# One of the experts' activation instructions moved from VectorE to ScalarE, and a slot's gate read as one sum

## The chip, the cores and the metric

The kernel runs on one core of a Trainium2 chip. Its time is the device time of that core, in microseconds (us). Three runs of the kernel before took 3082.26, 3086.06 and 3087.57 us; the median is 3086.06.

## The reference

Two transformer blocks over 512 tokens of width 1024, in float32. The first block mixes by attention and ends in a mixture of experts; the second block (two layers) mixes by three branches. The change lies in the experts of the first block. Each token is routed to 4 of 32 experts, and only the chosen ones count:

```python
def expert_block(args):
    xblk, e = args
    gu = xblk @ w_gate_up[e] + b_gate_up[e]
    gate = jnp.minimum(gu[:, :D_FF], SWIGLU_LIMIT)
    up = jnp.clip(gu[:, D_FF:], -SWIGLU_LIMIT, SWIGLU_LIMIT)
    act = (up + 1.0) * (gate * jax.nn.sigmoid(SWIGLU_ALPHA * gate))
    return act @ w_down[e] + b_down[e]
```

The limit is 7 and alpha 1.702. Each expert's result is scaled by the token's gate, a softmax over its four logits, and added to that token's row. The weights are 1024 x 2048 (gate and up) and 1024 x 1024 (down) per expert.

## The kernel before

**Products in split precision.** The matrix unit takes float32 rounded to a shorter mantissa. So every operand is split into a high part (a copy on ScalarE, line 49) and a low part (the rest, a subtraction on VectorE, line 50), and a product is three matmuls: high times low, low times high, high times high (lines 82 to 84). Each weight piece of 1 MB (`raw`, 128 x 2048) is loaded by a queue of SyncE, split into `whi` and `wlo`, and used by 12 matmuls of 512 columns. There are 8 buffers of `raw` and 4 each of `whi` and `wlo`, so `whi` of a piece can be made when the piece four places before has been used up.

**An expert.** Up to 96 token slots (NS) are served per expert. `place(e)` finds an expert's tokens: a one-hot matrix `poh` (line 765), four small matmuls and a sum give the row numbers `gi` (lines 777, 778), and four more matmuls with `VG`, which holds each gate as a high and a low part, give the two parts of every slot's gate in one PSUM tile `T` (line 782). Lines 784 and 785 bring the two parts to SBUF and add them into `gate`, which scales the expert's result much later (line 911). `gather` brings the tokens' rows, `prep` transposes and splits them. `gate_up(e, h, x)` computes one half of the hidden columns, 512 of them: `ps[0]` is the gate's product, `ps[1]` the up product, each of two weight pieces, each a PSUM bank `G` of its own begun by one bias matmul (line 849). Then comes the activation on 96 x 512 elements, and its result is transposed (line 892) and split for `down(e, h, ...)`, which multiplies it with two further weight pieces into two banks `Y`. An expert thus takes twelve pieces.

**The activation.** sigmoid is taken as half of 1 + tanh, and the half is put in at the split of the result. ScalarE computes relu(7 − gate) from `ps[0]` and from that the tanh; both take their constant from a column of a small tile `c7`. VectorE does four instructions: it bounds `up` (line 886), bounds the gate into a tile `gm` (line 887), computes (tanh + 1) times `gm` (line 888), and (up + 1) times that (line 889).

**Order.** The loop over experts writes `gate_up(e, 0)`, then `prep`, `gather` and `place` for later experts, then `down(e − 1, 1)`, `gate_up(e, 1)` and `down(e, 0)`. Each engine runs its instructions in a fixed order, but that order is not the written one: a planner goes through the program with its own account of time and gives an engine, whenever it comes free, the instruction that is ready and stands first in the program. The order of the whole program is planned anew whenever the program changes. The same function that reads the gates (`slots`) serves the overflow path, which runs only if an expert has more than 96 tokens.

Of the kernel before, what the change touches and what calls it, by code (L numbers as in the profile page):

```python
# [9 lines left out]
F32 = mybir.dt.float32  # L10
# [4 lines left out]
AF = mybir.ActivationFunctionType  # L15
ALU = mybir.AluOpType
AX = mybir.AxisListType
# [12 lines left out]
NS = 96  # L30
# [4 lines left out]
def f(t):  # L35
    return t.bitcast(F32)


class Kern:
# [729 lines left out]
    def slots(self, bank, oh, V, vg, gi, gate):  # L769

        nc = self.nc
        n = oh.shape[-1]
        p = bank[:n, :4]

        def find():
            for i in range(NT):
                nc.tensor.matmul(p[:, :2], lhsT=oh[:, i], rhs=V[:, i], start=i == 0, stop=i == NT - 1)
            return nc.vector.tensor_scalar(gi[:n], p[:, 0:1], BASE, self.spare[:n], op0=ALU.add, op1=ALU.min).ins

        def gates():  # L780
            for i in range(NT):
                nc.tensor.matmul(p[:, 2:], lhsT=oh[:, i], rhs=vg[:, i], start=i == 0, stop=i == NT - 1)
            g = self.small.tile([128, 2], F32, name="g2")
            nc.vector.tensor_copy(g[:n], p[:, 2:])
            nc.vector.tensor_add(gate[:n], g[:n, 0:1], g[:n, 1:2])
        return find, gates

    def gather(self, e):
# [4 lines left out]
    def moe_setup(self):  # L793

        nc, tc, a = self.nc, self.tc, self.a
        FF = 1024
        T = dict(reuse_waits="tile")
        self.ms = ExitStack()
        mc = self.mc = self.ms.enter_context(tc.tile_pool(name="mc", bufs=1, **T))
        xg = self.xg = [mc.tile([NS, D], F32, name=f"xg{n}") for n in range(2)]  # L800
        for t in xg:
            nc.gpsimd.memset(t, 0.0)
        self.mraw = self.ms.enter_context(tc.tile_pool(name="mraw", bufs=NE, **T))

        bias = self.bias = mc.tile([128, FF], F32R, name="bias")
        bt = self.mraw.tile([128, 2048], F32, name="bt", tag="raw")[:, :FF]
        for r in (0, 32):
            nc.sync.dma_start(bt[r:r + 32], a["b_gate_up"][:, :FF])  # L810
            nc.sync.dma_start(bt[64 + r:96 + r], a["b_gate_up"][:, FF:])
        nc.scalar.activation(bias, bt, AF.Copy)
        for r in (32, 96):
            nc.vector.tensor_sub(bias[r:r + 32], bt[r:r + 32], f(bias)[r:r + 32])

        esel = self.esel = mc.tile([128, 2, 32], F32R, name="esel")
        nc.gpsimd.memset(f(esel), 0.0)
        for r in range(0, 128, 32):
            nc.vector.tensor_copy(esel[r:r + 32, r // 64], self.ident[r:r + 32, r:r + 32])
        c7 = self.c7 = mc.tile([128, 2], F32, name="c7")  # L820
        nc.vector.memset(c7[:, 0:1], 7.0)
        nc.vector.memset(c7[:, 1:2], 0.851 * 7.0)
        self.gi = mc.tile([128, 32], I32, name="gi")
        self.gate = mc.tile([128, 32], F32, name="gate")

# [7 lines left out]
    def moe(self, ctx):  # L833


        nc, tc, a, mc = self.nc, self.tc, self.a, self.mc
        esel, bias, c7, xg = self.esel, self.bias, self.c7, self.xg
# [4 lines left out]
        mp = P("mp", 2, **T)  # L842
        self.wp, self.wk = (self.mraw, P("mhi", 4, **T), P("mlo", 4, **T)), 4
        psG, psY, psT = P("psG", 4, space=PSUM, **T), P("psY", 2, space=PSUM, **T), P("psTm", 2, space=PSUM, **T)
        gi, gate, gather = self.gi, self.gate, self.gather
        wgu, wdn = a["w_gate_up"], a["w_down"]

        def add_bias(ps, e, c):
            nc.tensor.matmul(ps, lhsT=esel[:, c // 2, e:e + 1].to_broadcast([128, NS]),
                             rhs=bias[:, c % 2 * 512:c % 2 * 512 + 512], start=True, stop=False)  # L850
# [20 lines left out]
        def gate_up(e, h, x):  # L871
            xh, xl = x
            ps = []
            for c in (h, 2 + h):
                W = self.weight(wgu[e, :, c * 512:c * 512 + 512], KT, 512)
                p = psG.tile([128, 512], F32, name="G")[:NS]
                add_bias(p, e, c)
                self.mm3(p, [((xh[:, k], xl[:, k]), W[k]) for k in range(KT)], start=False)
                ps.append(p)
            s = mp.tile([NS, 512], F32, name="sg", bufs=3)  # L880

            nc.scalar.activation(s, ps[0], AF.Relu, scale=-1.0, bias=c7[:NS, 0:1])
            nc.scalar.activation(s, s, AF.Tanh, scale=-0.851, bias=c7[:NS, 1:2])
            u = mp.tile([NS, 512], F32, name="up", bufs=3)
            g = mp.tile([NS, 512], F32, name="gm", bufs=2)
            nc.vector.tensor_scalar(u, ps[1], 7.0, -7.0, op0=ALU.min, op1=ALU.max)
            nc.vector.tensor_scalar(g, ps[0], 7.0, None, op0=ALU.min)
            nc.vector.scalar_tensor_tensor(s, s, 1.0, g, op0=ALU.add, op1=ALU.mult)
            self.act_dve = nc.vector.scalar_tensor_tensor(u, u, 1.0, s, op0=ALU.add, op1=ALU.mult).ins
            p = psT.tile([128, 512], F32, name="T", tag="T")[:, :4 * NS].rearrange("p (k s) -> p k s", k=4)  # L890
            for k in range(4):
                nc.tensor.transpose(p[:, k], u[:, k * 128:(k + 1) * 128], self.ident[:NS, :NS])
            th = mp.tile([128, 4, NS], F32R, name="ath", bufs=3)
            tl = mp.tile([128, 4, NS], F32R, name="atl", bufs=3)
            self.split(th, tl, p, 0.5)
            return th, tl
# [53 lines left out]
        for e in range(E):  # L950
            acts[e, 0] = gate_up(e, 0, x[e])
            if e + 1 < E:
                x[e + 1] = prep(e + 1)
                if e + 2 < E:
                    gather(e + 2)
                if e + 3 < E:
                    place(e + 3)
            if e == E - 4:
                gates_T()
            if e == E - 2:  # L960
                one_hot()
            if e:
                down(e - 1, 1, acts[e - 1, 1])
            acts[e, 1] = gate_up(e, 1, x[e])
            if e < E - 1:
                down(e, 0, acts[e, 0])
# [7 lines left out]
        g = gate[:NS, E - 1:E]  # L974
# [558 lines left out]
```

## Time and profile before

| | |
|---|---|
| median of three runs | 3086.06 us |
| the profiled execution | 3086.88 us |
| its span, first to last instruction | 3085.1 us |
| PE (TensorE's matmuls) busy | 2917.6 us, 95% |
| DVE (VectorE) busy | 2250.2 us, 73% |
| ACT (ScalarE) busy | 1737.4 us, 56% |
| mean granted clock of TensorE | 0.982 |

The experts' stage lies between about 700 and 1860 us of the span. In the rows, PE is the matmul engine and PEld its weight loads, and an instruction is written as what it writes, an arrow, and what it reads. L82 is line 82 of the kernel. A number in square brackets at the end of a timeline row is the idle time of the engine before it, with what ended the idle time. Times in a timeline row are the start and the duration in us. Consecutive instructions of one engine overlap a little, so the step from start to start is shorter than the duration.

### The profile page before, as it was taken

To read this page: it belongs to the slowest core of one execution; us is meant where nothing else is said; L and a number is where in the kernel's file an instruction comes from. 1 tells how busy PE (TensorE), PEld (TensorE's weight loads), DVE (VectorE), ACT (ScalarE), POOL (GpSimd) and SP (SyncE) were. 2 spreads that over 40 slices of the span, in tenths; PEclk is the share of its full clock that TensorE was granted. 3 is DMA by queue.
4 is the path that set the end of the run, shared out by engine and by line. 5 is a ranking of instruction groups with operands and counts; after the bars stand their busy time and mean duration, and the time that the engine had idled before them with its cause. 6 is when DMAs were issued, how large, how long until landed. Compare 5 with 4: busy or idle time off the path is not lost.

```text
span 3085.1 us, 39468 instructions
## 1 busy us (share of the span) xinstructions
PE 2917.6 (95%) x14226; PEld 2293.6 (74%) x14226; DVE 2250.2 (73%) x3789; ACT 1737.4 (56%) x2577; POOL 318.4 (10%) x316
## 2 busy tenths in 40 slices
PE   7999999979999999999999997999999979999998
PEld 6898878766777666666666665878887868888876
DVE  7765577668998999999999997554466585445664
ACT  5555545337777777777777774444454234444532
POOL 0000001001112111111111101011000020110000
PEclk9999999989999999999999999999999989999999
DMA  5122233469999999999999994433536433345262
GB/s 157 63 69 67 76 107 96 129 257 318 366 365 345 354 352 360 355 359 361 356 359 359 349 368 129 133 102 114 113 103 202 148 98 115 112 118 114 89 235 89
DMA packets 405833, 644.92 MB, mean 209 GB/s; under 512 B 23024, under 2 KB 150528, under 8 KB 405632
## 3 DMA queue, kind: packets, MB, share of 16 engines
q1 hardware_dynamic: 385808, 581.67, 56.6%
q0 software_dynamic: 19248, 58.58, 6.4%
q8 instruction: 114, 1.87, 0.3%
q10 hardware_dynamic: 576, 2.10, 0.2%
q14 instruction: 87, 0.71, 0.1%
HBM read 592.10 MB, written 54.36 MB: 210 GB/s over the span
## 4 chain that ended last, share of the span: by engine, by line
PE 74%; DVE 12%; issue 7%; ACT 3%; DMA 3%; SPq 0%; POOL 0%; POOLq 0%; ACTq 0%; DVEq 0%
PE M L82 6%; PE M L83 6%; PE G L82 6%; PE M L84 6%; PE G L84 6%; PE G L83 6%; PE F L82 5%; PE F L83 5%; PE F L84 5%; DVE wlo L50 5%; PE Y L82 4%; PE Y L83 3%; PE Y L84 3%; DMA raw<-in_w_in 1%; PE O L82 1%
## 5 line engine op out<-in xcount | busy, mean ns | idle before, releaser
L50 DVE TENSOR_TENSOR wlo<-raw,whi 128x2048 fp32r<-128x2048 f32 (+4 forms) x642 | 1161.9, 1821 | 274.0 <-ACT whi L49 269.8
L49 ACT ACTIVATE whi<-raw 128x2048 fp32r<-128x2048 f32 (+3 forms) x646 | 972.1, 1532 | 231.3 <-PE M L84 110.3
L82 PE MATMUL G<-wlo,exh 128*96 128x512 f32 x1024 | 410.0, 400 | 4.7 <-ACT exh L49 2.7
L83 PE MATMUL G<-whi,exl 128*96 128x512 f32 x1024 | 404.0, 395 | 1.9 <-DVE exl L50 1.9
L84 PE MATMUL G<-whi,exh 128*96 128x512 f32 x1024 | 403.8, 394 | 0.0
L82 PE MATMUL F<-xl,whi 128*128 128x512 f32 x768 | 311.3, 405 | 17.1 <-DVE fl L1228 10.0
L83 PE MATMUL F<-xh,wlo 128*128 128x512 f32 x768 | 305.3, 398 | 2.3 <-DVE wlo L50 2.3
L84 PE MATMUL F<-xh,whi 128*128 128x512 f32 x768 | 305.6, 398 | 0.0
L82 PE MATMUL M<-wlo,xh 128*128 128x512 f32 (+2 forms) x736 | 278.1, 380 | 12.4 <-POOL wlo L50 3.5
L83 PE MATMUL M<-whi,xl 128*128 128x512 f32 (+2 forms) x736 | 275.2, 374 | 0.0
L84 PE MATMUL M<-whi,xh 128*128 128x512 f32 (+2 forms) x736 | 274.0, 374 | 0.0
L84 PEld LDWEIGHTS G<-whi,exh 128*96 128x96 f32 x1024 | 165.7, 162 | 71.5
L82 PEld LDWEIGHTS G<-wlo,exh 128*96 128x96 f32 x1024 | 165.8, 162 | 70.6 <-ACT exh L49 3.0
L82 PE MATMUL Y<-wlo,ath 128*96 128x512 f32 x512 | 207.4, 405 | 10.6 <-DVE wlo L50 9.9
L83 PEld LDWEIGHTS G<-whi,exl 128*96 128x96 f32 x1024 | 165.7, 162 | 67.3 <-DVE exl L50 2.4
L83 PE MATMUL Y<-whi,atl 128*96 128x512 f32 x512 | 202.4, 395 | 0.1
L84 PE MATMUL Y<-whi,ath 128*96 128x512 f32 x512 | 201.8, 394 | 0.0
L82 PEld LDWEIGHTS M<-wlo,xh 128*128 128x128 f32 x736 | 164.4, 223 | 32.9 <-DVE wlo L50 4.9
L82 PEld LDWEIGHTS F<-xl,whi 128*128 128x128 f32 x768 | 146.0, 190 | 54.9 <-DVE fl L1228 13.5
L83 PEld LDWEIGHTS M<-whi,xl 128*128 128x128 f32 x736 | 165.0, 224 | 13.6
L84 PEld LDWEIGHTS M<-whi,xh 128*128 128x128 f32 x736 | 164.4, 223 | 14.1
L83 PEld LDWEIGHTS F<-xh,wlo 128*128 128x128 f32 x768 | 146.2, 190 | 32.0 <-DVE wlo L50 3.0
(479 smaller groups left out, 5095.3 us busy)
## 6 DMA issues: line engine op xcount, KB each, us to landing
raw<-in_w_gate_up SPq DMA_DIRECT2D x256, 1024.0 KB, 7.0
raw<-in_w_down SPq DMA_DIRECT2D x124, 1024.0 KB, 8.2
raw<-in_w_in SPq DMA_DIRECT2D x154, 512.0 KB, 4.0
GZ<-fl POOLq DMA_DIRECT2D x80, 256.0 KB, 2.4
raw<-in_w_out SPq DMA_DIRECT2D x24, 512.0 KB, 3.9
raw<-in_w_branch SPq DMA_DIRECT2D x24, 512.0 KB, 4.4
gt<-GZ SPq DMA_DIRECT2D x48, 256.0 KB, 3.1
raw<-in_w_in SPq DMA_DIRECT2D x32, 256.0 KB, 3.1
```

The lines of the kernel that those rows point to most:

```text
L49: self.last_act = nc.scalar.activation(hi, src, AF.Copy)
L50: self.last_dve = (eng or nc.vector).tensor_sub(lo, src, f(hi))
L82: nc.tensor.matmul(out, lhsT=ah, rhs=bl, start=start and i == 0, stop=False)
L83: nc.tensor.matmul(out, lhsT=al, rhs=bh, start=False, stop=False)
L84: self.last_mm = nc.tensor.matmul(out, lhsT=ah, rhs=bh, start=False, stop=stop and i == n - 1)
```

## The change

The 1 of 1 + tanh is added by a third instruction on ScalarE (an Identity with the constant 1 as its bias, a new column of `c7`). VectorE bounds the gate and multiplies it with 1 + tanh in one instruction, which reads `ps[0]` itself; the tile `gm` is gone. The activation has three instructions on ScalarE and three on VectorE, where it had two and four. In `slots` the two parts of a gate are summed in one instruction that reads PSUM, instead of a copy and an addition.

```diff
@@ -780,9 +780,7 @@
         def gates():
             for i in range(NT):
                 nc.tensor.matmul(p[:, 2:], lhsT=oh[:, i], rhs=vg[:, i], start=i == 0, stop=i == NT - 1)
-            g = self.small.tile([128, 2], F32, name="g2")
-            nc.vector.tensor_copy(g[:n], p[:, 2:])
-            nc.vector.tensor_add(gate[:n], g[:n, 0:1], g[:n, 1:2])
+            nc.vector.reduce_sum(gate[:n], p[:, 2:], axis=AX.X)
         return find, gates
@@ -817,9 +815,10 @@
-        c7 = self.c7 = mc.tile([128, 2], F32, name="c7")
+        c7 = self.c7 = mc.tile([128, 3], F32, name="c7")
         nc.vector.memset(c7[:, 0:1], 7.0)
         nc.vector.memset(c7[:, 1:2], 0.851 * 7.0)
+        nc.vector.memset(c7[:, 2:3], 1.0)
@@ -881,11 +880,10 @@
             nc.scalar.activation(s, ps[0], AF.Relu, scale=-1.0, bias=c7[:NS, 0:1])
             nc.scalar.activation(s, s, AF.Tanh, scale=-0.851, bias=c7[:NS, 1:2])
+            nc.scalar.activation(s, s, AF.Identity, bias=c7[:NS, 2:3])
             u = mp.tile([NS, 512], F32, name="up", bufs=3)
-            g = mp.tile([NS, 512], F32, name="gm", bufs=2)
+            nc.vector.scalar_tensor_tensor(s, ps[0], 7.0, s, op0=ALU.min, op1=ALU.mult)
             nc.vector.tensor_scalar(u, ps[1], 7.0, -7.0, op0=ALU.min, op1=ALU.max)
-            nc.vector.tensor_scalar(g, ps[0], 7.0, None, op0=ALU.min)
-            nc.vector.scalar_tensor_tensor(s, s, 1.0, g, op0=ALU.add, op1=ALU.mult)
             self.act_dve = nc.vector.scalar_tensor_tensor(u, u, 1.0, s, op0=ALU.add, op1=ALU.mult).ins
```

## Rows read from the trace of the kernel before

**Rows 1.** Windows, one early expert and a late pair: us, busy (count), clock, DMA

```profile
core 0: us, PE busy (x) PEld busy (x) DVE busy (x) ACT busy (x) POOL busy (x), PEclk, DMA share, GB/s
840.58:876.85 36.27, 36.27 (x173) 25.81 (x172) 34.18 (x29) 28.00 (x23) 5.01 (x2) 1.00 1.04 364
...
967.36:1041.64 74.28, 73.42 (x347) 51.26 (x346) 68.73 (x56) 55.20 (x45) 10.24 (x4) 1.00 1.03 357
```

**Rows 2.** Waits, 960 to 1730 us: us in total, times, longest

```profile
ACT sg L882 <- PE G L84: 69.9, 42, 3.3
...
PEld Y L82 <- DVE wlo L50: 29.0, 51, 1.2
```

**Rows 3.** Groups by line, 700 to 1860 us: busy us, mean ns

```profile
L888 DVE SCALAR_TENSOR_TENSOR sg<-sg,gm 96x512 f32<-96x512 f32 x64 | 43.8, 684 | 2.7 <-ACT sg L883 0.2
...
L887 DVE TENSOR_SCALAR gm<-G 96x512 f32<-96x512 f32 x63 | 42.9, 680 | 0.0
...
L883 ACT ACTIVATE sg<-sg,c 96x512 f32<-96x512 f32 x64 | 46.0, 719 | 1.1
```

**Rows 4.** Timeline of ACT, an early expert

```profile
840.58 0.69 ACT L882 ACTIVATE sg<-G,c 96x512 f32<-96x512 f32 x1 [1.03 <-PE G L84]
841.17 1.91 ACT L49 ACTIVATE whi<-raw 128x2048 fp32r<-128x2048 f32 x1
842.97 0.71 ACT L883 ACTIVATE sg<-sg,c 96x512 f32<-96x512 f32 x1
```

**Rows 5.** Timeline of a late half, kind B: ACT, DVE, PE

```profile
1061.00 0.68 ACT L882 ACTIVATE sg<-G,c 96x512 f32<-96x512 f32 x1 [3.26 <-PE G L84]
1061.72 0.72 ACT L883 ACTIVATE sg<-sg,c 96x512 f32<-96x512 f32 x1
1062.35 5.52 ACT L49 ACTIVATE whi<-raw 128x2048 fp32r<-128x2048 f32 x3
...
1064.29 2.30 DVE L50 TENSOR_TENSOR wlo<-raw,whi 128x2048 fp32r<-128x2048 f32 x1 [1.09 <-ACT whi L49]
...
1066.64 0.48 PE L82 MATMUL Y<-wlo,ath 128*96 128x512 f32 x1
```

**Rows 6.** Timeline of a late half, kind D: DVE, PE

```profile
1026.97 2.29 DVE L50 TENSOR_TENSOR wlo<-raw,whi 128x2048 fp32r<-128x2048 f32 x1 [0.63 <-ACT whi L49]
...
1029.32 0.48 PE L82 MATMUL Y<-wlo,ath 128*96 128x512 f32 x1
```

**Rows 7.** Timeline of a late half, kind A: PE, DVE

```profile
1044.87 0.42 PE L782 MATMUL T<-VG,poh 128*96 128x2 f32 x4
...
1045.59 0.15 DVE L784 COPY g<-T 96x2 f32<-96x2 f32 x1
...
1046.12 0.68 DVE L888 SCALAR_TENSOR_TENSOR sg<-sg,gm 96x512 f32<-96x512 f32 x1
1046.72 2.28 DVE L50 TENSOR_TENSOR wlo<-raw,whi 128x2048 fp32r<-128x2048 f32 x1
...
1049.06 0.47 PE L82 MATMUL Y<-wlo,ath 128*96 128x512 f32 x1 [0.65 <-DVE wlo L50]
```

**Rows 8.** Timeline of a late half, kind C, and the tenth one's relu: ACT, DVE, PE

```profile
1005.33 0.69 ACT L882 ACTIVATE sg<-G,c 96x512 f32<-96x512 f32 x1 [0.84 <-PE G L84]
...
1006.68 1.90 ACT L49 ACTIVATE whi<-raw 128x2048 fp32r<-128x2048 f32 x1
...
1009.02 2.28 DVE L50 TENSOR_TENSOR wlo<-raw,whi 128x2048 fp32r<-128x2048 f32 x1
...
1011.35 0.47 PE L82 MATMUL Y<-wlo,ath 128*96 128x512 f32 x1
...
1013.96 0.39 PE L84 MATMUL Y<-whi,ath 128*96 128x512 f32 x1
1014.18 0.40 PE L849 MATMUL G<-bias,esel 128*96 128x512 f32 x1
...
1014.75 0.47 PE L82 MATMUL Y<-wlo,ath 128*96 128x512 f32 x1 [0.17 <-DVE wlo L50]
...
1673.83 0.69 ACT L882 ACTIVATE sg<-G,c 96x512 f32<-96x512 f32 x1 [0.84 <-PE G L84]
```

## The prediction, made before the changed kernel was run

> **What bounds the kernel now.** I read the page's busy shares first, then the windows of the experts' stage, cut at the activation of one expert and of a later one, then that stage's waits, and last the timeline around the activation. The windows say that the stage runs at two paces [rows 1]. An early expert takes 36.27 us, and TensorE (PE) is busy for all of it. Two late experts together take 74.28 us, 37.14 each, so something costs each late expert 0.87 us more. The granted clock is 1.00 in both rows, so it is not the clock. In neither stretch is VectorE (DVE) or ScalarE (ACT) full: in the late one they are busy 68.73 and 55.20 of 74.28 us.
>
> The waits tell who is late in the late stretch [rows 2]: PE's weight loads for the first matmul of a down product wait for the low part `wlo` of its weights, 51 times, 29.0 us in all, and ACT waits 69.9 us for PE before an activation starts. So there is a ring: PE ends a gate's product, ACT runs relu and tanh on it and only then makes the high part `whi` of the next weights, DVE makes `wlo` from that, and PE takes `wlo` up. I call the first weight piece of a down product W4. The loads from memory do not stand in this ring: no row of ACT or DVE that I read in that view waits for one.
>
> A late pair of experts has four halves of the activation, and each ends at a "Y" matmul.
> - **B** [rows 5]: relu at 1061.00, tanh at 1061.72, whi(4) at 1062.35, wlo(4) at 1064.29 after DVE idled 1.09 us for that whi, its end at 1066.59, Y at 1066.64. DVE has time to spare; ACT's chain sets Y.
> - **D** [rows 6]: the same, DVE idle 0.63 us for whi(4), wlo(4) ends at 1029.26, Y at 1029.32.
> - **A** [rows 7]: DVE runs without a gap, wlo(4) ends at 1049.00, Y at 1049.06 with 0.65 us of PE idle. DVE sets Y.
> - **C** [rows 8]: wlo(4) ends at 1011.30 and Y starts at 1011.35. A second Y at 1014.75 comes behind a bias matmul of 1014.18; with matmuls 0.22 to 0.23 apart (1013.96 to 1014.18) it could have started at 1014.41 and lost 0.34 to wlo(5).
>
> The first relu of kind C is at 1005.33 and the tenth at 1673.83 [rows 8], nine steps of 74.28, so there are ten such pairs.
>
> **The change part by part.** *Identity on ACT.* Its nearest row is the tanh, same shape, same source, same kind of bias: 719 ns [rows 3]. It reads what tanh writes, as tanh reads what relu writes: tanh starts 0.72 behind a relu of 0.68, so 0.04 after its end [rows 5]. The Identity then starts 0.76 behind tanh, and what follows it, which does not depend on it, 0.63 behind the Identity, as whi(4) does behind tanh. There are 64. Where it stands in ACT's order decides. In the late kinds nothing but a short copy stands between relu and tanh, so W4 was not yet to be had in the planner's account when relu was done; I take it that it still is not when tanh is done, and the Identity goes ahead of whi(4). Then whi(4) is 0.76 later (bounds 0.63, without the 0.13 that dependence adds, and zero, if whi(4) goes first). In B and D wlo(4) already waits for it and Y for wlo(4), so each loses 0.76: +1.52 per pair.
>
> *One instruction fewer on DVE.* Gone is the minimum `gm` (680 ns); the product that took 684 ns [rows 3] stays one instruction, with one input from PSUM instead of SBUF. The two rows read one and the other and cost the same, so I take 0.68 for it, a step of 0.60 (1046.12 to 1046.72) [rows 7]. In B and D the saving falls into time in which DVE idled and is worth nothing. In A it is worth a step of 0.60 unless something else is late next, and something is: the gate's sum, which stands before wlo(4), needs the small matmuls that start at 1044.87 and take 0.42 [rows 7]. It can start at about 1045.33 instead of 1045.59, then one-hot, product and wlo(4) follow, so Y comes 0.26 earlier. Bounds 0 and −0.65 (all of PE's idle); I take −0.25. In C the Identity moves whi(4) from 1006.68 to 1007.44, it ends at 1009.34, and wlo(4) starts at 1009.37 instead of 1009.02, although DVE has less to do: the first Y goes to 1011.70. The second is then ready at 1014.41 + 0.35 = 1014.76, and wlo(5), one step of 0.60 nearer to wlo(4) than before, is done by then: 1014.75 stays. Zero; bounds −0.34 (the Identity behind whi(4)) and +0.35.
>
> *The gate as one sum.* One short DVE instruction per expert goes. The sum itself I price as the copy, 0.15 us [rows 7]; at worst it is as long as a 96x512 instruction, 0.68, which in A alone would cost 0.5, 5 us over ten pairs. Nothing waits for the gate before the down product is done. Zero.
>
> *A third constant.* One memset before the stage, one element per partition, no longer than the copy of 0.15 us, once. Zero.
>
> *The early experts.* There whi goes between relu and tanh [rows 4], PE is busy throughout, and ACT only 28.00 of 36.27 us [rows 1]: twice 0.76 us fits into 8.3 us of idle. Zero; if that cover were gone it would be B's price, 1.52 an expert. The bank of the gate's product is held longer, until the new product has read it instead of the minimum, 0.76 + 0.63 us or so against an expert's 36 us before that bank is used again. Zero. The halves behind the tenth pair are left out of the sum; each that has B's form adds 0.76, and for a handful of them I widen the upper end by 4.
>
> Sum: ten pairs × (0.76 + 0.76 − 0.25 + 0) = 10 × 1.27 = +12.7 us on the profiled 3086.88, 3099.6. That execution lies 0.82 us above the median of the runs shown, so 3098.8, in round numbers 3098, against 3086.06.
>
> **Two rules weighed.** The windows show PE busy 73.42 of 74.28 us, idle 0.86, while the pace against two early experts shows 1.74 lost [rows 1]. The Trainium skill, Trainium Kernel Development and Optimization, Performance Expectations, says that matmul busy time tells little of how near a kernel is to its peak, because matmuls are pipelined. By busy time ten pairs could give back 8.6 us, by the pace 17.4; the trace agrees with the rule.
>
> Tanh costs 719 ns on ACT and the product 684 ns on DVE [rows 3], 35 ns apart. The Trainium skill, ScalarE: Activation LUTs, Rules for kernel authors, says to keep additions and multiplications on VectorE, because it is faster per element. By these durations 64 moves would cost 2 us; the trace bears the direction out, and the place in the ring makes it more.
>
> **Rivals.**
> 1. *The relief comes through* (not slower). The planner puts whi(4) ahead of the Identity in B and D, so nothing is lost there, and A and C keep their savings. For it: in the early experts it put a whi into the gap between two dependent activations [rows 4]. Against: in the late kinds it did not. It decides at whether W4 is to be had before tanh ends. Price: 10 × (−0.65 − 0.34) = −9.9, 3076 on the median's scale; if every wait of the late pairs goes, −17.4, 3069.
> 2. *The two sides cancel.* Only one of B and D is delayed, with A at its −0.25: 10 × (0.76 − 0.25) = +5.1, 3091; with A at −0.65 it is +1.1, 3087. For it: the kinds reach the relu with different idle time before it, 3.26 us in B and 0.84 in C [rows 5, 8], so W4 need not be equally late in all. Against: the order after tanh is the same in them.
> 3. *The change does not do what it says, because the order is planned anew everywhere.* Experts could go from the early pace to the late one or back, 0.87 us each [rows 1], three of them 2.6 us either way. It widens every case and has no place of its own.
>
> **How the numbers follow.** A difference under 0.2%, 6.2 us, is no change here. Forecast (slower, 3093 to 3105): 0.50. Rival 1 (faster, 3069 to 3080): 0.25. Rival 2 (3081 to 3092): 0.25. So faster 0.25, same 0.25, slower 0.50. Of rival 1 the lower 0.1 is left out and of the forecast about as much at the top: 3074 to 3104.
>
> **What would show it.** Right: ACT's order relu, tanh, Identity, whi in the late halves; Y in B and D some 0.8 us behind a PE that was ready; a late pair near 75.6 us; DVE's busy time down by some 44 us, ACT's up by 46. Wrong: a whi between tanh and Identity in B and D, a late pair under 74.28 us, or the early pace held for more experts.

## The result and the profile after

Five runs of the changed kernel have a median of 3101.23 us (3099.84 to 3108.56), five of the kernel before beside them 3086.06 (3082.26 to 3087.57). The ratio is 1.0058, 95% interval 1.0042 to 1.0074: slower, by 15 us of the medians. Forecast were 3098 and slower. The profiled execution took 3100.15 us with a span of 3098.4, 13.3 us more than before.

The size is about right, the place mostly not. I cut both spans at the same instructions: the first relu, the third (one expert later), the fifteenth, the fifty-sixth, the first `yh` behind the last expert, and the first projection of the second block that VectorE normalises.

| us | before | after | difference |
|---|---|---|---|
| first block, to the first relu | 698.0 | 696.1 | −1.9 |
| first expert | 33.2 | 37.3 | +4.1 |
| six early experts | 218.2 | 218.1 | −0.1 |
| 20.5 late experts | 760.7 | 764.4 | +3.8 |
| the last halves, to `yh` | 163.6 | 165.5 | +1.9 |
| turn to the second block | 89.7 | 92.1 | +2.4 |
| second block | 1121.7 | 1124.9 | +3.2 |

The forecast had all of its 12.7 us in the late experts; they gave 3.8. The granted clock of TensorE has a large share in the rest: by the two traces it took 56.6 us of the span before and 64.0 of the span after (each stretch of time, times what its granted clock lacks to 1), 7.4 of the 13.3 us.

The page's first part shows the move near the forecast 44 and 46 us: VectorE (DVE) 41.7 us less busy, ScalarE (ACT) 41.6 more.

```profile
PE 2934.5 (95%) x14226; PEld 2296.8 (74%) x14226; DVE 2208.5 (71%) x3694; ACT 1779.0 (57%) x2641; POOL 304.6 (10%) x316
```

The windows that answer to [rows 1], an early expert and a late pair: 36.36 against 36.27 us, and 74.54 against 74.28. PE's idle time in the pair is only 0.35 us, though against two early experts it loses 1.82. The Trainium skill, Trainium Kernel Development and Optimization, Performance Expectations, calls matmul busy time a bad measure of how near a kernel is to its peak, because matmuls are pipelined. These rows agree, as those of before did.

```profile
842.37:878.73 36.36, 36.36 (x173) 25.84 (x172) 33.08 (x26) 29.24 (x24) 5.43 (x2) 1.00 1.05 366
1231.30:1305.84 74.54, 74.19 (x345) 51.25 (x344) 66.16 (x51) 57.93 (x48) 7.13 (x4) 1.00 1.02 354
```

The waits from 960 to 1730 us, beside [rows 2]: ACT waits less for PE (46.2 us for 69.9), DVE now waits 52.4 us for a high part, and the weight loads of Y wait 82 times instead of 51, for 34.0 us: twice in each half, once for each of the two pieces of the down product. The gate's sum, now one reduction, waits 30.6 us for PE.

```profile
DVE wlo L50 <- ACT whi L49: 52.4, 61, 2.0
ACT sg L881 <- PE G L84: 46.2, 41, 1.4
...
PEld Y L82 <- DVE wlo L50: 34.0, 82, 0.6
DVE gate L783 <- PE T L782: 30.6, 21, 1.5
```

The groups that answer to [rows 3]: the product that reads the gate in PSUM costs 680 ns, the Identity 707.

```profile
L883 ACT ACTIVATE sg<-sg,c 96x512 f32<-96x512 f32 x64 | 45.3, 707 | 0.1
...
L885 DVE SCALAR_TENSOR_TENSOR sg<-G,sg 96x512 f32<-96x512 f32 x64 | 43.5, 680 | 2.5 <-ACT sg L883 2.3
```

**The late halves.** The four kinds of [rows 5 to 8] have become two, one for each half of every expert. First the half whose relu is at 1249.54, on ACT, DVE and PE.

```profile
1249.54 0.69 ACT L881 ACTIVATE sg<-G,c 96x512 f32<-96x512 f32 x1 [1.44 <-PE G L84]
1250.26 0.72 ACT L882 ACTIVATE sg<-sg,c 96x512 f32<-96x512 f32 x1
1250.88 1.90 ACT L49 ACTIVATE whi<-raw 128x2048 fp32r<-128x2048 f32 x1
1252.69 0.71 ACT L883 ACTIVATE sg<-sg,c 96x512 f32<-96x512 f32 x1
...
1252.82 2.29 DVE L50 TENSOR_TENSOR wlo<-raw,whi 128x2048 fp32r<-128x2048 f32 x1 [2.01 <-ACT whi L49]
1255.03 0.68 DVE L885 SCALAR_TENSOR_TENSOR sg<-G,sg 96x512 f32<-96x512 f32 x1
...
1256.95 4.48 DVE L50 TENSOR_TENSOR wlo<-raw,whi 128x2048 fp32r<-128x2048 f32 x2
...
1254.65 0.39 PE L84 MATMUL G<-whi,exh 128*96 128x512 f32 x1
1255.16 0.47 PE L82 MATMUL Y<-wlo,ath 128*96 128x512 f32 x1
...
1258.03 0.63 PE L848 MATMUL G<-bias,esel 128*96 128x512 f32 x2
...
1258.82 0.49 PE L864 MATMUL T<-ident,xg 96*128 96x96 f32 x4
1259.28 0.47 PE L82 MATMUL Y<-wlo,ath 128*96 128x512 f32 x1
```

The order is relu, tanh, whi(4), Identity: the Identity stands behind the piece that Y needs. From relu to Y it takes 5.62 us, as in B before (5.64, [rows 5]). But Y starts 0.51 behind the matmul before it, where 0.23 is the step, so PE loses 0.28. In B a bias matmul of 0.23 stood there and filled the gap; here the planner has put both bias matmuls behind the first piece of the down product (1258.03).

The Identity itself shows at the second piece. DVE idles 2.01 us before wlo(4), but the product that reads tanh cannot run there as it did in B before (at 1062.51, ahead of the wlo at 1064.29), because it needs the Identity, which ends at 1253.40. So it stands behind wlo(4), at 1255.03, and with it the rest of the activation, ahead of wlo(5) at 1256.95. The second piece's Y comes 0.46 behind its predecessor, where 0.28 is the step without a wait (in e5 below, 1251.83 to 1252.11).

The other half, relu at 1231.30:

```profile
1234.35 0.16 DVE L783 TENSOR_REDUCE gate<-T 96x1 f32<-96x2 f32 x1 [1.53 <-PE T L782]
1234.42 0.54 DVE L765 TENSOR_TENSOR poh<-i,rk 128x384 fp32r<-128x384 f32 x1
1234.89 2.28 DVE L50 TENSOR_TENSOR wlo<-raw,whi 128x2048 fp32r<-128x2048 f32 x1
...
1236.77 0.39 PE L84 MATMUL G<-whi,exh 128*96 128x512 f32 x1
1237.22 0.48 PE L82 MATMUL Y<-wlo,ath 128*96 128x512 f32 x1
```

DVE has time to spare, and spends it at the head of its queue: the gate's sum waits 1.53 us for PE and holds up the one-hot and wlo(4) behind it, although whi(4) had ended at 1234.55. Y comes 0.45 behind its predecessor, 0.22 lost. The second piece's Y, at 1240.62, is 0.09 late.

**The first expert.** PE has no other expert's product to turn to there. On ACT the Identity stands behind a high part, then PE waits twice:

```profile
709.06 1.91 ACT L49 ACTIVATE whi<-raw 128x2048 fp32r<-128x2048 f32 x1
710.86 0.72 ACT L883 ACTIVATE sg<-sg,c 96x512 f32<-96x512 f32 x1
...
714.38 0.70 PE L82 MATMUL Y<-wlo,ath 128*96 128x512 f32 x2 [1.72 <-ACT ath L52]
718.67 0.90 PE L864 MATMUL T<-ident,xg 96*128 96x96 f32 x4 [2.20 <-DVE atl L53]
```

Behind these two waits TensorE's granted clock is 0.63 from 716 to 722 us and 0.80 in the six us after; in the kernel before, where PE also waited twice there, 0.23 and 1.82 us, it is 0.76 and 0.95. Over the whole first expert it is 0.91 and 0.95, which is 3.4 and 1.7 us lost. So of the 4.1 us about 1.9 are longer waits and up to 1.7 the clock. The two do not go strictly together: in the kernel with one memset more (e3 below), behind waits of 0.21 and 1.83 us, the clock stays at 1.00, and its first expert takes 31.7 us. Two windows of after, then one of before and one of e3:

```profile
716.00:722.00 6.00, 3.80 (x12) 2.59 (x13) 4.23 (x5) 0.49 (x1) 0.00 (x0) 0.63 1.05 383
722.00:728.00 6.00, 6.00 (x28) 4.29 (x27) 1.92 (x2) 2.76 (x3) 1.44 (x1) 0.80 0.15 56
```

```profile
716.00:722.00 6.00, 4.43 (x16) 2.96 (x17) 6.00 (x7) 1.02 (x2) 0.00 (x0) 0.76 1.03 366
```

```profile
716.00:722.00 6.00, 5.08 (x24) 3.60 (x25) 6.00 (x8) 2.04 (x2) 0.00 (x0) 1.00 1.03 379
```

**The last half.** DVE waits 2.33 us for the Identity there, but the Identity does not set the end. Behind the product DVE waits another 1.04 us for `up`, and PE's transposes wait 1.59 us for DVE as they did before; from the relu to them it is 7.13 us, and 7.09 before. What differs is behind them: matmuls that took 0.40 us in before take 0.63, and the granted clock of the last halves is 0.99 where it was 1.00, some 1.7 us of their 165.5. The rows of after, then two of before:

```profile
1866.87 0.69 DVE L885 SCALAR_TENSOR_TENSOR sg<-G,sg 96x512 f32<-96x512 f32 x1 [2.33 <-ACT sg L883]
1868.59 0.69 DVE L886 TENSOR_SCALAR up<-G 96x512 f32<-96x512 f32 x1 [1.04 <-PE G L84]
...
1870.15 0.52 PE L890 MATMUL T<-ident,up 96*128 96x96 f32 x4 [1.59 <-DVE up L887]
...
1872.11 0.63 PE L84 MATMUL Y<-whi,ath 128*96 128x512 f32 x1
```

```profile
1863.64 0.52 PE L892 MATMUL T<-ident,up 96*128 96x96 f32 x4 [1.59 <-DVE up L889]
...
1865.22 0.40 PE L84 MATMUL Y<-whi,ath 128*96 128x512 f32 x1
```

### The profile page after: what moved, and what is told of

Its sections match the earlier page's. It is cut to its first block, busy times and chain, and to the rows that moved or that the text cites. A ratio compares the mean times of both kernels' runs of the same rounds, so it can differ in the third digit from the quotient of the medians.

```text
span 3098.4 us, 39391 instructions
## 1 busy us (share of the span) xinstructions
PE 2934.5 (95%) x14226; PEld 2296.8 (74%) x14226; DVE 2208.5 (71%) x3694; ACT 1779.0 (57%) x2641; POOL 304.6 (10%) x316
## 5 line engine op out<-in xcount | busy, mean ns | idle before, releaser
L82 PEld LDWEIGHTS M<-wlo,xh 128*128 128x128 f32 x736 | 164.9, 224 | 34.1 <-POOL wlo L50 4.9
L83 PEld LDWEIGHTS M<-whi,xl 128*128 128x128 f32 x736 | 165.2, 224 | 15.0 <-DVE xl L50 1.5
L1000 POOL DMA_INDIRECT X<-y,gi x31 | 86.5, 2790 | 883.4 <-ACT y L909 883.4
```

Source lines behind the costliest of these rows:

```text
L82: nc.tensor.matmul(out, lhsT=ah, rhs=bl, start=start and i == 0, stop=False)
L83: nc.tensor.matmul(out, lhsT=al, rhs=bh, start=False, stop=False)
L1000: self.nc.gpsimd.indirect_dma_start(out=self.X1[:, :], out_offset=bass.IndirectOffsetOnAxis(ap=rows, axis=0), in_=y, in_offset=None, bound ...
```

## The experiments

The theory that the experiments were to test, formed after the two traces: the Identity costs latency where nothing covers it, at the first and the last expert; in the late halves the relief of DVE and the Identity nearly cancel; the rest is order laid anew, or the clock. Its rivals are the prediction's (the Identity costs 0.76 in the ring) and that any edit moves this program as much. The cut of each profiled run, in us, with the ratio to the kernel before on the same chip; "late" is the 20.5 late experts, "stage" the sum of first to last:

| kernel | ratio, 95% | first block | first | late | last | stage | turn | second block |
|---|---|---|---|---|---|---|---|---|
| before | | 698.0 | 33.2 | 760.7 | 163.6 | 1175.7 | 89.7 | 1121.7 |
| after | 1.0058 (1.0042–1.0074) | 696.1 | 37.3 | 764.4 | 165.5 | 1185.3 | 92.1 | 1124.9 |
| e1_gate_sum | 1.0028 (1.0018–1.0038) | 698.0 | 33.1 | 759.3 | 163.4 | 1174.1 | 93.4 | 1131.1 |
| e2_act_only | 1.0044 (1.0032–1.0056) | 697.0 | 37.4 | 766.2 | 164.4 | 1186.0 | 92.1 | 1121.9 |
| e3_one_memset | 0.9996 (0.9987–1.0005) | 697.3 | 31.7 | 760.5 | 164.9 | 1175.4 | 87.3 | 1123.9 |
| e4_one_ahead | 1.0082 (1.0069–1.0096) | 698.7 | 37.1 | 771.5 | 168.1 | 1194.8 | 91.9 | 1125.2 |
| e5_no_one | 0.9984 (0.9975–0.9993) | 697.7 | 31.8 | 749.2 | 162.0 | 1161.1 | 93.2 | 1122.1 |
| e6_act_more | 1.0046 (1.0032–1.0059) | 698.0 | 37.6 | 766.6 | 165.2 | 1187.7 | 92.0 | 1125.3 |
| e7_piece_first_after | 1.0010 (1.0001–1.0020) | 696.9 | 37.3 | 753.0 | 163.4 | 1171.7 | 91.8 | 1132.1 |
| e8_regroup | 1.0062 (1.0048–1.0076) | 699.9 | 36.7 | 764.7 | 165.5 | 1184.8 | 92.0 | 1131.2 |
| e9_sigmoid | 0.9976 (0.9965–0.9987) | 699.0 | 31.8 | 749.2 | 162.1 | 1161.2 | 93.1 | 1124.7 |
| e10_sigmoid_piece | 0.9996 (0.9988–1.0005) | 698.8 | 33.4 | 753.8 | 160.0 | 1165.2 | 94.0 | 1125.7 |
| e11_first_expert | 1.0048 (1.0035–1.0061) | 700.6 | 32.4 | 764.4 | 166.3 | 1182.0 | 91.8 | 1125.7 |
| e12_sigmoid_turn | 0.9974 (0.9965–0.9983) | 699.0 | 31.9 | 749.3 | 162.0 | 1161.2 | 91.1 | 1127.6 |

Three kernels with as many instructions in a half (e5, e9, e12) have the same stage within 0.2 us. The late experts ran at a granted clock of 1.00 in every kernel of the table, so that column can be read to fractions of a us. The columns beside it hold the clock as well: e3, which runs the experts of before unchanged, has a first expert 1.5 us shorter (1.00 for 0.95) and last halves 1.3 us longer (0.99 for 1.00). "Second block" holds still more of it, as will be seen.

**Each part alone.**

```diff
# e1_gate_sum: before, with
-            nc.vector.tensor_copy(g[:n], p[:, 2:])
-            nc.vector.tensor_add(gate[:n], g[:n, 0:1], g[:n, 1:2])
+            nc.vector.reduce_sum(gate[:n], p[:, 2:], axis=AX.X)
# e2_act_only: after, with the reverse of this
# e3_one_memset: before, with
-        c7 = self.c7 = mc.tile([128, 2], F32, name="c7")
+        c7 = self.c7 = mc.tile([128, 3], F32, name="c7")
+        nc.vector.memset(c7[:, 2:3], 1.0)
```

> The kernel before with the gate sum alone (one reduction for the copy and the addition, 38 VectorE instructions fewer), the activation as before. By the prediction (the sum is worth nothing, its bound 5 us the other way): 3086, within 3. By the theory formed from the two traces (the added instruction costs at the first and the last expert and a little in each late pair; the rest of the difference is the order laid anew in other stages): 3081 to 3091, and what it moves lies outside the activation. By the rival that any edit of the program moves the time by as much as the change did: over 8 us from 3086 either way.

> The changed kernel with the old gate sum (copy and addition): the activation's edit alone. By the prediction and by the theory from the traces: all of the loss, 3097 to 3103. If the gate's reduction, which stands ahead of a low part on VectorE and waits for TensorE in the changed kernel's trace, is a share of the loss: 3090 to 3096. If the order laid anew decides: anywhere from 3080 to 3105, and with other steps lengthened than in the changed kernel.

> The kernel before with one VectorE instruction of some 60 ns added in the experts' setup (a third constant that nothing reads). It takes nothing itself. By the prediction: 3086, within 1. If the order that is laid anew after an edit matters in this program: more than 2 us from 3086 either way, spread over stages that the edit doesn't touch; over 8 us would put the whole difference of the change within such moves.

Medians 3097.13, 3099.44 and 3085.66 us. The activation alone has all of the stage's loss (e2). The memset leaves the median where it was, so not every edit moves the time. The gate sum alone (32 instructions fewer on the pages, not 38) was a surprise: its own stage is 1.6 us shorter, and yet the run is some 9 us longer, all of it behind the experts: 3.7 us in the turn and 9.4 in the second block of the profiled run. Both the prediction (within 3 us) and the theory (3081 to 3091) missed that.

**The second block** has another reason than its order. TensorE's 5292 instructions there stand in the same order in before, e3, e6 and e8, and in e1 two places differ; it took 1121.7, 1123.9, 1125.3, 1131.2 and 1131.1 us. In after, e2 and e7, which share another order (1488 places differ from before), it took 1124.9, 1121.9 and 1132.1. So each order covers about the whole spread. What differs is how long the same matmuls take (PE is busy 9.9 us longer in a block that is 9.5 us longer) and the granted clock. These are the windows of that block for before and e8, and the same goes for e1 (0.97 and 1131.10). With one digit more the clock is 0.977 and 0.972, which takes 25.8 and 31.2 us of the block: 5.4 of the 9.5. The rest of the longer matmuls is not explained.

```profile
1963.40:3085.10 1121.70, 1056.81 (x5294) 883.88 (x5292) 623.21 (x1453) 483.55 (x1020) 101.23 (x161) 0.98 0.43 125
```

```profile
1976.70:3107.90 1131.20, 1066.75 (x5294) 889.86 (x5292) 623.17 (x1453) 483.45 (x1020) 101.21 (x161) 0.97 0.42 124
```

Runs of one kernel differ in the same way: e1 took 3090 to 3092 us in two runs at a mean clock of 0.981 and 0.982, and 3096 to 3099 in seven at 0.977 to 0.979. The changed kernel's +3.2 us in the second block lie within this spread. Why e1 ran at the lower clock so often isn't settled; even its two shortest runs are some 7 us above e3's at that clock (3082 to 3086).

**Both sides of the activation.**

```diff
# e5_no_one: after, without
-            nc.scalar.activation(s, s, AF.Identity, bias=c7[:NS, 2:3])
# e6_act_more: before, with
+            nc.scalar.activation(s, s, AF.Identity, bias=c7[:NS, 2:3])
-            nc.vector.scalar_tensor_tensor(s, s, 1.0, g, op0=ALU.add, op1=ALU.mult)
+            nc.vector.scalar_tensor_tensor(s, s, 0.0, g, op0=ALU.add, op1=ALU.mult)
```

> The changed kernel without the added ScalarE instruction: the one is not added at all (the gate's product is with tanh instead of 1 + tanh), VectorE has the changed kernel's three instructions and the one gate sum. What is left is the relief of VectorE. By the prediction (early experts and three of four late halves don't wait for VectorE; its rival puts the relief at 17 us at most): 3074 to 3088. By the theory from the traces: the first expert and the last half get their time back, 3083 to 3090. If any edit moves the time as much: anywhere from 3075 to 3100.

> The kernel before (four VectorE instructions in a half, old gate sum) with the one added on ScalarE as in the change, and VectorE adding zero in its place: the cost of the ScalarE instruction without the relief. By the prediction (ScalarE's place costs 12.7 us and the relief of VectorE hides behind other waits): 3096 to 3104. By the theory from the traces (latency at the first and last expert, 5 to 6 us, plus the late pace): 3094 to 3106, with the step from the first to the third relu over 735 us long against 731.2. If the relief did matter: over 3106.

Medians 3081.88 and 3103.04. e5 leaves out the 1 and so computes another activation; it is there for its time alone, and lies under the 3083 to 3090 of the theory. e6 lies in the ranges of the prediction and of the theory. With the parts before, the stage reads as a square: neither 1175.7; Identity alone +12.0 (e6); relief and gate sum alone −14.6 (e5), of which the sum is −1.6 (e1); all three +9.6. The clock is in these numbers (it took 1.7 us of the stage in before and e1, none in e5, 3.4 in e2, 5.1 in after and e6). In the late experts, where it is 1.00 throughout, the square reads: Identity alone +5.9, relief and gate sum alone −11.5, of which the sum is −1.4, all three +3.8. So the two sides don't add up to the sum: there the relief is worth 10.1 us without the Identity and 0.4 with it (e6 to e2), and the Identity costs 15.2 us on the relieved kernel and 5.9 on the other. By the durations, 707 for 680 ns in 64 places, it would be 1.7 in the whole stage. The Trainium skill, ScalarE: Activation LUTs, Rules for kernel authors, advises VectorE for additions because it is faster per element (its figure is for bf16). The direction agrees, the size is that of the place.

Why the relief pays in e5, one late half with its relu at 1240.01, on ACT, DVE and PE:

```profile
1241.36 5.51 ACT L49 ACTIVATE whi<-raw 128x2048 fp32r<-128x2048 f32 x3
...
1241.49 0.69 DVE L884 SCALAR_TENSOR_TENSOR sg<-G,sg 96x512 f32<-96x512 f32 x1 [0.20 <-ACT sg L882]
1243.29 2.29 DVE L50 TENSOR_TENSOR wlo<-raw,whi 128x2048 fp32r<-128x2048 f32 x1 [1.12 <-ACT whi L49]
...
1245.38 0.40 PE L848 MATMUL G<-bias,esel 128*96 128x512 f32 x1
1245.64 0.48 PE L82 MATMUL Y<-wlo,ath 128*96 128x512 f32 x1
```

The ring is as long as ever (5.63 us), but up product and one bias matmul cover it: Y comes 0.26 behind the bias, 0.03 lost. The product runs at 1241.49, in the time in which DVE would wait for whi(4) anyway, so that wlo(5) follows at 1246.19 and the second piece's Y waits for nothing. In e5 and e9 the product stands ahead of wlo(4) in all four late halves; in after, e2 and e6 it stands behind it in all four. No run moves the product alone, so that this place is what the Identity costs is read from these rows and not shown by itself. Three of four late halves lose 0.06 us or less at the first Y, and the pair takes 73.13 us:

```profile
1222.12:1295.25 73.13, 73.05 (x347) 51.28 (x346) 66.33 (x51) 55.00 (x44) 10.26 (x5) 1.00 1.03 362
```

**The Identity's place.**

```diff
# e4_one_ahead: after, in down()
+                self.behind = (self.ident_act,) if c == 0 and 7 <= e < E - 1 else ()
                 W = self.weight(wdn[e, h * 512:h * 512 + 512, c * 512:c * 512 + 512], 4, 512, ...)
# e7_piece_first_after: after, in gate_up(), relu behind the next down product's first piece
+                    wd[nxt] = w_down(*nxt, 0)
+                    first.enter_context(tc.issue_after(self.last_act.ins))
                 nc.scalar.activation(s, ps[0], AF.Relu, scale=-1.0, bias=c7[:NS, 0:1])
# e11_first_expert: after, weights of expert 0's second half behind its first half's Identity
+            self.behind = (self.ident_act,) if e == 0 else ()
             acts[e, 1] = gate_up(e, 1, x[e])
```

> The changed kernel with one order imposed from expert 7 on: the first weight piece of each down product (high part) is issued on ScalarE only behind the added instruction of the half at hand, which is the place that the prediction took for it. By the prediction (0.76 us in two of the four kinds of late half): late pair near 75.6 us, the run some 10 us over the changed kernel, 3108 to 3114. By the theory that the ring has slack where the changed kernel shows VectorE waiting for TensorE: under 4 us more, 3101 to 3105. If the order laid anew decides: no relation to the imposed place, 3085 to 3115 with other steps moved as well.

> The changed kernel with the opposite order: the first weight piece of the next down product is split on ScalarE before the half's relu, so that the ring of the late halves (product, relu, tanh, high part, low part, product) is cut. By the prediction's reading of the ring: every pair runs at the early pace, 72.6 us, and the run is 10 to 20 us shorter than the changed kernel, 3080 to 3091. If a piece can't be ready that early (its buffer or its transfer), the relu waits for it instead: no gain or a loss, 3100 to 3125.

> The changed kernel with one order imposed at the very first expert only: the weights of its second half are split behind the added instruction of its first half, so that relu, tanh and the added instruction follow each other where the changed kernel puts two high parts of 1.8 us among them. By the theory that this place cost 4 us of the 13: the step from the first to the third relu falls from 37.3 to 33 to 35.5 us, the run by 2 to 4 us, 3096 to 3100. If the split weights are what TensorE needs next: the step stays at 37 or grows, 3100 to 3106. If the order laid anew decides: steps elsewhere move by more than this one.

Medians 3112.34, 3092.02 and 3101.93. In e4 the prediction's place was imposed, and its price is there. The half whose relu is at 1254.31, on ACT, DVE and PE, and the window of a late pair:

```profile
1255.79 0.72 ACT L883 ACTIVATE sg<-sg,c 96x512 f32<-96x512 f32 x1
1256.42 5.51 ACT L49 ACTIVATE whi<-raw 128x2048 fp32r<-128x2048 f32 x3
...
1258.35 2.29 DVE L50 TENSOR_TENSOR wlo<-raw,whi 128x2048 fp32r<-128x2048 f32 x1 [1.12 <-ACT whi L49]
...
1259.65 0.40 PE L848 MATMUL G<-bias,esel 128*96 128x512 f32 x1
1260.70 0.47 PE L82 MATMUL Y<-wlo,ath 128*96 128x512 f32 x1 [0.65 <-DVE wlo L50]
```

```profile
1235.99:1311.23 75.24, 73.36 (x345) 51.27 (x344) 66.67 (x51) 58.12 (x48) 6.89 (x4) 1.00 1.02 350
```

From relu to Y it is 6.39 us against 5.62, 0.77 more where 0.76 was forecast, and PE loses 0.82 in spite of the bias matmul. The other half, where DVE had waited for PE, loses 0.46. The late pair is 75.24 (forecast 75.55). So the price of the place was right, and the changed kernel has another place. In e7 the opposite order takes 11.4 us off the late experts of the changed kernel (36.7 us each), which shows that the ring sets their pace; it does not reach the early 36.3, and the run misses the 3080 to 3091 that was expected by 1 us. In e11 the first expert's step falls to 32.4 us as expected, but the third relu is no earlier (733.0 against 733.3 us): the first one came 4.6 us later. That run says nothing for the theory of the first expert. The table sorts by PE's waits there and the granted clock: 36.7 to 37.6 us where PE waits 3.9 to 4.9 us at 0.91 (all other kernels with the Identity, and e8, which has none), 33.1 to 33.4 where it waits 1.8 to 2.1 at 0.95 (before, e1, e10), 31.7 to 31.9 with the same waits at 1.00 (e3, e5, e9, e12). So the Identity goes with the longer waits, but is not alone in making them.

**A version without the one.** Two ways to drop a DVE instruction and add none on ACT:

```diff
# e8_regroup: (up + 1) through the bias, one instruction behind tanh
+        nc.vector.tensor_scalar(bt[64:], bt[64:], 1.0, None, op0=ALU.add)
+            nc.vector.tensor_scalar(u, ps[1], 8.0, -6.0, op0=ALU.min, op1=ALU.max)
+            nc.vector.scalar_tensor_tensor(u, ps[0], 7.0, u, op0=ALU.min, op1=ALU.mult)
+            self.act_dve = nc.vector.scalar_tensor_tensor(u, s, 1.0, u, op0=ALU.add, op1=ALU.mult).ins
# e9_sigmoid: after, without the Identity, and
-            nc.scalar.activation(s, s, AF.Tanh, scale=-0.851, bias=c7[:NS, 1:2])
+            nc.scalar.activation(s, s, AF.Sigmoid, scale=-1.702, bias=c7[:NS, 1:2])
-            self.split(th, tl, p, 0.5)
+            self.split(th, tl, p, 1.0)
# e10_sigmoid_piece: e9 with the edit of e7
# e12_sigmoid_turn: e9; the third norm's square ahead of two pieces, the fourth's ahead of two more
+            third = self.norms[2][0]
-                (self.fw, (sq,), nc.gpsimd)] * 2 + [(None, (hi, lo), None)] * 2)
+                (self.fw, (sq,), nc.gpsimd)] * 2 + [(None, (hi, lo, third), None)] * 2)
+            self.behind = (self.norms[3][0],)
             W = self.weight(w_in[:, 1536:1952], KT, 416)
```

> Another way to take an instruction from VectorE: the one of (up + 1) goes into the up bias (rows 64 to 127 of the bias get 1 added once; the clip is then from -6 to 8), the gate's bound and its product with up run while ScalarE has relu and tanh, and behind tanh stands one instruction, (tanh + 1) times that product. Nothing is added on ScalarE. By the theory that the added latency between relu and the transposes is what the change lost at the first and last expert: 3078 to 3086, the first expert shorter than before. By the prediction's ring (ScalarE's relu, tanh and high part as before): 3082 to 3087. If the order laid anew decides: 3075 to 3100.

> The changed kernel with sigmoid in place of tanh, so that no one has to be added anywhere: (1 + tanh(x)) / 2 is sigmoid(2x); relu and sigmoid on ScalarE, three VectorE instructions, the one gate sum, no factor of a half at the split. ScalarE and VectorE have as many instructions in a half as in the kernel without the one, which measured 3081.9 (0.9984 of before). By the theory that the ScalarE instruction alone took the relief away: the same, 3076 to 3085, late pair 73.1 against 74.28, all of the gain inside the experts' stage. By the rival that it depends on how the program is laid out: 3085 to 3105. A table load at the stage's start and one behind it may add a few us outside the pairs.

> The kernel with sigmoid, and the first weight piece of each down product split ahead of the half's relu. By the prediction's ring (relu, function, high part, low part, down product): the late pair falls from 73.1 towards the early pace, 72.6, and the run by another 3 to 8 us, 3068 to 3080. By what the same order did to the changed kernel (late pair 74.56 to 73.3): with less on ScalarE there is less to win, 0 to 3 us. If the relu now waits for the piece: 3080 to 3095.

> The kernel with sigmoid (3080.0, turn from the last expert to the second block 93.1 us) with ScalarE's order of the kernel before imposed on that turn: the third norm's square ahead of two weight pieces and the fourth's ahead of the two pieces of 832 columns. In the kernel before the turn takes 89.7, in the one with a memset more 87.3, both in that order; in the changed kernel and the five others with the other order 91.7 to 93.4. If the order of these four pieces is what the turn lost: 87 to 90 in place of 93.1, the run 3075 to 3079. If it is the granted clock or anything else ahead of the turn: 91.5 to 94, the run 3078 to 3083.

Medians 3107.91, 3080.04, 3085.21 and 3079.70. e8 failed: it shortens the chain behind tanh, but `up` ends last, and behind it now stand three DVE instructions instead of two. In the last half of e8 DVE waits 3.71 us for `up`, then does the three, and PE's transposes wait 2.45 for them (1.59 in before and after). Its run lies outside all three ranges. Its late experts run at the changed kernel's 37.3 us without an Identity, and its rows show the same places: all three DVE instructions need `up` and stand behind wlo(4), the first Y comes 0.45 and 0.51 us behind a `G` matmul with no bias matmul between, and one second Y in two is late, by 0.4. So this pace is that of the places, not of the Identity as such.

```profile
1871.09 0.69 DVE L884 TENSOR_SCALAR up<-G 96x512 f32<-96x512 f32 x1 [3.71 <-PE G L84]
...
1873.51 0.52 PE L889 MATMUL T<-ident,up 96*128 96x96 f32 x4 [2.45 <-DVE up L886]
```

e9 beats both kernels: by the ratios 0.24% under before and 0.8% under after. A sigmoid takes as long as a tanh did (720 ns for 719), and the table for it is loaded once in the stage (a row of ACT; below it the window of a late pair); one more load of 1.28 us follows in the second block, at 1999.5, which the other kernels do not have.

```profile
701.49 1.28 ACT L881 ACT_TABLE_LOAD   x1
```

```profile
1223.45:1296.59 73.14, 73.06 (x347) 51.28 (x346) 66.36 (x51) 55.04 (x45) 10.29 (x5) 1.00 1.02 356
```

Of its 14.5 us in the stage 3.4 are given back in the turn and 3.0 in the second block. e10 adds nothing: the fixed order costs 4.6 us in the late experts, where little was left to win.

The turn: in before ACT takes the third norm's square ahead of two weight pieces, in e1, after and e9 it takes the two pieces first (the square is at 1893.15 and the pieces at 1894.19 in before; at 1901.64 and 1899.75 in after). e12 imposes before's order on e9: 91.1 us for 93.1. That is less than the 3 to 6 us expected and lies between the two cases named, at a granted clock of 0.89 (e9 0.91, before 0.94). But before and e3, with one order and one clock (0.94), took 89.7 and 87.3, so that 2 us of order are not shown, and the median doesn't show them either (3079.70 for 3080.04). What the turn's 2.4 us are in the changed kernel stays open.

## Why the prediction was right or wrong

- **What bounds the late experts**: right, but not all of it. Y waits for wlo(4) in every late half of the changed kernel, and moving whi(4) either way (e4, e7) moves the late experts by 7.1 and 11.4 us. The second piece, wlo(5), which the prediction priced in one half of four, is late in every half too.
- **The step that failed: "the Identity goes ahead of whi(4)"**, and with it the term 10 × 1.27 = 12.7 us. The planner put whi(4) straight behind tanh in both halves, as rival 1 had it. The 20.5 late experts cost 3.8 us, 0.28 us for a pair as the medians of the steps show (74.56), where the term had 1.27. I had argued from "it still is not to be had when tanh is done"; the row at 1250.88 refutes it.
- **The price of that place**, 0.76: right, 0.77 in e4.
- **Rival 1** had the order right and its gain wrong: with the Identity behind whi(4) the relief should have come through, −9.9 us. It did not, for reasons that I had not named: both halves settle where the first Y is 0.2 to 0.3 us late, in one because the gate's sum stands ahead of wlo(4) waiting for PE, in the other because the bias matmul that covered the ring has gone elsewhere; and the second Y is 0.1 to 0.2 us late, because the product that reads the Identity has moved from the idle time ahead of wlo(4) to behind it. These are readings of the rows; no run undoes them one by one. Without the Identity, the relief pays more than rival 1's price (late pair 73.13: 1.15 a pair, of which the gate's sum is 0.13, for 0.99 priced and at most 1.74).
- **"B and D: ACT's chain sets Y"**: half right. In both, Y started 0.30 behind a bias matmul (at 1066.34 and 1029.02), where the step is 0.23, so chain and PE arrived together. A chain that is just covered has nothing to lose by rows of waits, and everything by one more instruction.
- **The early experts, zero**: right (36.36 for 36.27).
- **The first and the last expert**: not in the sum; the 4 us that I added to the upper end for late halves were meant for others. They cost 4.1 and 1.9 us, and the turn 2.4, which together replace what the pairs did not lose. Of these the longer waits at the first expert, some 1.9 us, go with the change; much of the rest goes with the granted clock, for which the prediction had no term. That the total came out near the forecast is luck.
- **The gate's sum, zero**: right in its stage (−1.6 us, 153 ns an instruction as priced); the runs' 9 us behind the stage were not foreseen and are explained in part.
- **Replanning, 2.6 us either way**: too small. The second block alone moves by up to 10 us at one and the same order, with a clock of 0.972 to 0.980 and longer matmuls; this is not replanning, and the prediction had no room for it.

## What to carry to other kernels

Price an instruction by its place in its engine's queue, and first look whether the chain is covered: here, in the late experts, one of 0.71 us on ACT costs 15 us or 6, and one of 0.68 less on DVE is worth 10 or 0.4, each by what the other engine does. Ask also what an added step makes wait: a product that could run in idle time may have to move behind the work that is waited for. An addition that changes engines still has to be done; a function that contains it (sigmoid for (1 + tanh)/2) takes it off both. Before explaining half a per cent, cut the span at a few fixed instructions and read the granted clock of each part: the total agreed here while its parts did not.

## What the runs showed of the hardware

A stage of one and the same order of TensorE's instructions differs by 0.8% between two executions, 1121.7 and 1131.2 us, all of it in the time of the matmuls; a granted clock of 0.977 and 0.972 accounts for 5.4 of the 9.5 us. The 0.63 of 716 to 722 us in the changed kernel, after waits of 1.72 and 2.20 us, means that three quarters of that stretch ran at the lower of the clock's two levels, 1.2 GHz ((1 − 0.63) / 0.5). One and the same pair of waits does not always bring the fall: behind 0.23 and 1.82 us in before the clock of that stretch is 0.76, behind 0.21 and 1.83 us in e3 it is 1.00, and that is 1.5 us of the first expert. In the turn, at a granted 0.94 and 0.89, the matmul that ends PE's wait of 3.5 us for a low part takes 0.51 us in before, at 1896.00, and 0.80 in after, at 1902.64. A reduction of 96 x 2 elements takes 153 ns, as a copy of the same shape did (0.15, [rows 7]).
